# Layer A's inputs for quarters 2 to 4 from a transposed copy of x, normed in place on VectorE

## The chip, the cores and the metric

The kernel runs on one core of a Trainium2 chip. The metric is the device time of one execution in microseconds (us). An engine is named by what it is: TensorE (PE in the rows, PEld for its weight loads), VectorE (DVE), ScalarE (ACT), GpSimd (POOL) and SyncE (SP), whose queue issues all DMAs of this kernel.

## The reference

A trunk of two layers over 2048 tokens of width 1024, in f32. Layer A, which the change touches, begins with a norm over the features and a modulation, and everything after it reads that result with the features on the partitions:

```
def rms_norm(x, g):
    y = x * lax.rsqrt(jnp.mean(x * x, axis=-1, keepdims=True) + EPS)
    return y * g
def gmlp_layer(x, ...):
    h = rms_norm(x, norm_g) * (1 + scale) + shift
    u, v, z = jnp.split(h @ w_in, 3, axis=-1)
    ...
    return x + gate * (y @ w_out)
```

The shared K and V (h @ w_kv of layer A's output) and layer B (queries, attention over three dilations, w_out) follow.

## The kernel before

The tokens go in four quarters of 512, Q = 0 to 3, and each quarter runs through layer A, the K and V products (kv) and layer B's products (q, z) before the next. A product of 128x512 of output is summed in f32 precision out of three passes: operand and weight are split in a high and a low part (`split`, lines 272 and 273: ScalarE copies the high part, VectorE subtracts for the low one), and TensorE does high by high, high by low and low by high (`mm3`, line 301). One part of a quarter's work on the next quarter's input is recorded as a generator, a filler, whose steps are set between the matmuls at a rate (`tick`); each step's instructions then stand in their engines' queues at the place where it was taken, and a scheduler may still move them. Engines run their queues in order, and so does SP.

The inputs of layer A for quarters 1, 2 and 3 (the second to the fourth; named by Q in tiles such as h_a and pt_a) come from such fillers:

- `make_h(1, ...)` for quarter 2 and `make_h(0, ...)` for quarter 1 are both appended during Q = 0, the first beside the K and V products and the second from `ahead`, beside layer B's.
- `make_hA(nxt, 3, ...)` for quarter 3 is appended during Q = 2, beside layer B's products.

Each loads its four x tiles (128 tokens by 1024, 512 KB each) into one tile `xa` of a pool with one buffer, squares them on ScalarE in halves (`sqj`, line 897 or 1052), gets the reciprocal root on GpSimd (`rstd_of`, line 263), scales the x tiles by it on ScalarE (line 905), and then transposes them on TensorE, 32 transposes of 128x128 to a quarter (`pt_a`, line 915, or 861 in `norm_T`). VectorE applies the modulation as it copies the transposes from PSUM (line 917 or 870, 128x256 at a time), and the result h goes to DRAM (`hh`, `hd`). For quarters 1 and 3 it is also split: ScalarE copies the high part and GpSimd subtracts for the low one (lines 922 and 923, 872 and 876).

Four buffers of a pool `cb` with five, tag xin, hold the residual tiles xr of the quarter's own output while layer A's output product (pd_o, with weights w_o) fills them; their squares (xo, line 1358), the norm's reciprocal root r_b, the scaling on VectorE (line 1373) and the transposes `pt_b` (line 981) lead to hkh and hkl, the operands of kv. The residual goes to DRAM by `x1d`.

Of the kernel before, what the change touches and what calls it, by code (L numbers as in the profile page):

```python
# [34 lines left out]
@with_exitstack  # L35
def trunk(ctx, tc, out, x, c, a_ada_w, a_ada_b, a_norm_g, a_w_in, a_sgu_g, a_w_spatial,
          a_b_spatial, a_w_out, kv_ada_w, kv_ada_b, kv_norm_g, w_kv, k_norm_g, b_ada_w,
          b_ada_b, b_norm_g, b_w_in, b_q_norm_g, b_w_out, w_uz):
    nc = tc.nc
    x = x[0]  # L40
    out = out[0]
# [10 lines left out]
    bp = ctx.enter_context(tc.tile_pool(name="bp", bufs=2))  # L52
    sp = ctx.enter_context(tc.tile_pool(name="sp", bufs=4))
# [16 lines left out]
    hd = dp.tile([2, P, KT, 256], F32, name="hd")  # L70
    hh = dp.tile([2, P, KT, QT], F32, name="hh")
# [776 lines left out]
    def bigr(nm):  # L848
        return big.tile([P, KT, QT], F32R, tag="big", name=nm)

    def norm_T(xts, pr, outs, nm, ks=range(0, KT, 2), act=False):

        tok = slice(pr * 256, pr * 256 + 256)
        pts = {}
        for oi, (hh, hl, a, b) in enumerate(outs):
            for k2 in ks:
                if oi == 0:
                    pts[k2] = pst(f"pt_{nm}{k2}").rearrange("p (k t) -> p k t", k=2)
                    for kk in range(2):
                        for i in range(2):  # L860
                            last = nc.tensor.transpose(pts[k2][:, kk, i * P:(i + 1) * P],
                                                       xts[i][:, (k2 + kk) * P:(k2 + kk + 1) * P], ident)
                h = evt(f"h_{nm}{k2}_{oi}").rearrange("p (k t) -> p k t", k=2)
                for kk in range(2):
                    k = k2 + kk
                    if act or (oi == 1):
                        nc.scalar.activation(h[:, kk, :], pts[k2][:, kk, :], AF.Identity,
                                             scale=a[:, k:k + 1], bias=b[:, k:k + 1])
                    else:
                        nc.vector.tensor_scalar(h[:, kk, :], pts[k2][:, kk, :], a[:, k:k + 1],  # L870
                                                b[:, k:k + 1], ALU.mult, ALU.add)
                nc.scalar.activation(hh[:, k2:k2 + 2, tok], h, AF.Copy)
                if len(outs) == 1:
                    nc.sync.dma_start(hd[pr, :, k2:k2 + 2, :], h)
                e = nc.vector if oi == 0 and len(outs) > 1 else nc.gpsimd
                e.tensor_tensor(hl[:, k2:k2 + 2, tok], h,
                                hh[:, k2:k2 + 2, tok].bitcast(F32), ALU.subtract)
        return last

    def op_tile(nm, pool=big):  # L880
        t = pool.tile([P, 2, 4, QT], F32R, tag="big", name=f"op{nm}")
        return t[:, 0], t[:, 1]

    def make_h(half, aff, ops):

        Q = 1 + half
        xb = one.tile([P, TPQ, D], F32, tag="big", name=f"xa{Q}")
        xts = [xb[:, t, :] for t in range(TPQ)]
        for t in range(TPQ):
            nc.sync.dma_start(xts[t], x[(Q * TPQ + t) * P:(Q * TPQ + t + 1) * P, :])  # L890
        yield
        sq = sp.tile([P, 16], F32, tag="sqa", bufs=1, name=f"sqa{Q}")
        for t in range(TPQ):
            yield
            for h in range(2):
                j = evt(f"sqj{Q}{t}{h}")
                nc.scalar.activation(j, xts[t][:, h * 512:(h + 1) * 512], AF.Square,
                                     accum_out=sq[:, 4 * h + t:4 * h + t + 1])
        yield
        nc.gpsimd.tensor_tensor(sq[:, 8:12], sq[:, 0:4], sq[:, 4:8], ALU.add)  # L900
        r = rstd_of(sq[:, 8:12], TPQ, D, f"r_a{Q}")
        yield
        yield
        for t in range(TPQ):
            nc.scalar.activation(xts[t], xts[t], AF.Copy, scale=r[:, t:t + 1])
            yield
        for pr in range(2):
            tok = slice(pr * 256, pr * 256 + 256)
            for k2 in range(0, KT, 2):
                pt = pst(f"pt_a{Q}{pr}{k2}").rearrange("p (k t) -> p k t", k=2)  # L910
                h = evt(f"h_a{Q}{pr}{k2}").rearrange("p (k t) -> p k t", k=2)
                for kk in range(2):
                    k = k2 + kk
                    for i in range(2):
                        nc.tensor.transpose(pt[:, kk, i * P:(i + 1) * P],
                                            xts[2 * pr + i][:, k * P:(k + 1) * P], ident)
                    nc.vector.tensor_scalar(h[:, kk, :], pt[:, kk, :], aff[0][:, k:k + 1], aff[1][:, k:k + 1],
                                            ALU.mult, ALU.add)
                nc.sync.dma_start(hh[half, :, k2:k2 + 2, tok], h)
                if ops:  # L920
                    hi, lo = (o[:, k2 % 4:k2 % 4 + 2, tok] for o in ops[k2 // 4])
                    nc.scalar.activation(hi, h, AF.Copy)
                    nc.gpsimd.tensor_tensor(lo, h, hi.bitcast(F32), ALU.subtract)
                yield

    def sums_h(ops, n):

# [111 lines left out]
    def make_hA(res, Q, aff):  # L1039
        hA = (bigr(f"hAh{Q}"), bigr(f"hAl{Q}"))  # L1040
        res["hA"] = hA
        xb = one.tile([P, TPQ, D], F32, tag="big", name=f"xa{Q}")
        xts = [xb[:, t, :] for t in range(TPQ)]
        for t in range(TPQ):
            nc.sync.dma_start(xts[t], x[(Q * TPQ + t) * P:(Q * TPQ + t + 1) * P, :])
        yield
        sq = sp.tile([P, 16], F32, tag="sqa", bufs=1, name=f"sqa{Q}")
        for t in range(TPQ):
            yield
            for h in range(2):  # L1050
                j = evt(f"sqj{Q}{t}{h}")
                nc.scalar.activation(j, xts[t][:, h * 512:(h + 1) * 512], AF.Square,
                                     accum_out=sq[:, 4 * h + t:4 * h + t + 1])
        yield
        nc.gpsimd.tensor_tensor(sq[:, 8:12], sq[:, 0:4], sq[:, 4:8], ALU.add)
        r = rstd_of(sq[:, 8:12], TPQ, D, f"r_a{Q}")
        yield
        yield
        for t in range(TPQ):
            nc.scalar.activation(xts[t], xts[t], AF.Copy, scale=r[:, t:t + 1])  # L1060
            yield
        for pr in range(2):
            for k2 in range(0, KT, 2):
                norm_T(xts[2 * pr:2 * pr + 2], pr, [hA + aff], f"a{Q}_{pr}_", (k2,))
                yield

    def sums_A(Q, hA, m):

# [804 lines left out]
    outs = []  # L1873
# [187 lines left out]
    hA, m, sqv, ends = begin(affa)  # L2061
# [13 lines left out]
    for Q in range(NQ):  # L2075
# [40 lines left out]
        if Q == 2:  # L2116
            hA = nxt["hA"]
# [28 lines left out]
```

## Time and profile before

| what | us |
|---|---|
| runs of before: lowest, median, highest | 2903.33, 2909.21, 2909.3 |
| the profiled execution | 2910.12 |
| its span in the profile | 2908.3 |
| TensorE busy | 2851.9 (98%) |
| VectorE, ScalarE, GpSimd busy | 76%, 56%, 28% |

The span runs from the first to the last instruction in the profile of one execution, at a granted clock of 0.998. Busy time is the union of an engine's instructions. TensorE's idle time is thus only 56 us in all, spread over the span.

### The profile page before, as it was taken

How to read it: one execution, taken by the hardware profiler on the slowest of the kernel's cores; microseconds unless marked ns; L12 is line 12 of the kernel's file. 1: busy time of each engine (PE TensorE's matmuls, PEld its weight loads, DVE VectorE, ACT ScalarE, POOL GpSimd, SP SyncE). 2: the span in 40 equal slices, each digit the busy share in tenths (PEclk: the TensorE clock that was granted, in tenths of full speed). 3: DMA queues.
4: the chain of work that ended last, by engine and by line, in shares of the span. 5: the costliest groups of instructions: out<-in, count | busy, mean ns of one | idle time of the engine just before them, and what ended most of it. 6: DMA issues, size and time to landing. Idle time of an engine off the chain costs nothing.

```text
span 2908.3 us, 45236 instructions
## 1 busy us (share of the span) xinstructions
PE 2851.9 (98%) x14450; PEld 2386.6 (82%) x14450; DVE 2205.5 (76%) x4104; ACT 1639.2 (56%) x3335; POOL 819.7 (28%) x1085
## 2 busy tenths in 40 slices
PE   8999999999999999999999999999999999999999
PEld 5788888877888888878888788888888888888887
DVE  6887667786696789967777877789779676888782
ACT  4324345666556666545654557667666357776441
POOL 1067422330031025003315134115335121122312
PEclk9999999999999999999999999999999999999999
DMA  9899856887874555797888787955447867789653
GB/s 320 289 334 343 286 194 206 273 297 268 293 270 161 200 170 181 241 330 240 301 289 298 238 302 258 299 181 168 151 129 259 319 217 232 235 274 334 223 172 111
DMA packets 388209, 718.74 MB, mean 247 GB/s; under 512 B 42010, under 2 KB 121084, under 8 KB 387588
## 3 DMA queue, kind: packets, MB, share of 16 engines
q1 hardware_dynamic: 387972, 715.87, 73.1%
q8 instruction: 114, 1.87, 0.3%
q14 instruction: 123, 1.01, 0.1%
HBM read 541.52 MB, written 174.20 MB: 246 GB/s over the span
## 4 chain that ended last, share of the span: by engine, by line
PE 79%; DVE 6%; DMA 5%; ACT 4%; issue 4%; POOL 1%; SPq 0%; POOLq 0%; ACTq 0%; DVEq 0%
PE pd_kv L301 8%; PE po L1844 4%; PE pd_o L301 3%; PE pd_v L301 2%; PE pd_z L345 2%; PE pd_z L344 2%; PE pd_z L343 2%; PE pd_u L343 2%; PE pd_u L345 2%; PE pd_u L344 2%; PE pd_o3a L301 1%; PE pd_v3b L301 1%; DMA qt<-qd 1%; PE pf L2035 1%; PE pf L2037 1%
## 5 line engine op out<-in xcount | busy, mean ns | idle before, releaser
L301 PE MATMUL pd_kv<-w_kv,hkh 128*128 128x512 f32 x672 | 209.4, 392 | 2.2 <-DVE w_kv L273 2.1
L1844 PEld LDWEIGHTS po<-kv,pT 128*128 128x128 f32 x1200 | 148.8, 193 | 15.1 <-POOL pT L1819 4.4
L1844 PE MATMUL po<-kv,pT 128*128 128x128 f32 x1200 | 152.2, 277 | 6.3 <-ACT pT L1690 2.5
L301 PEld LDWEIGHTS pd_kv<-w_kv,hkh 128*128 128x128 f32 x672 | 125.0, 188 | 29.3 <-DVE w_kv L273 2.9
L301 PE MATMUL pd_kv<-w_kv,hkl 128*128 128x512 f32 x336 | 130.9, 390 | 0.0
L1607 POOL TENSOR_SCALAR s_q<-s_q 128x4 f32<-128x4 f32 x96 | 25.3, 264 | 350.5 <-DVE s_q L1606 276.3
L1784 ACT ACTIVATE pr<-pr,stat,rt 128x256 f32<-128x256 f32 (+1 forms) x192 | 104.2, 544 | 27.0 <-DVE stat L1778 18.9
L1463 POOL TENSOR_SCALAR vc<-vc,rvh 128x256 f32<-128x256 f32 x64 | 66.8, 1060 | 182.4 <-DMA vc<-vh 128.0
L272 ACT ACTIVATE w_q<-raw_q 128x512 fp32r<-128x512 f32 x144 | 88.2, 627 | 46.8 <-PE pd_kv L301 12.4
L273 DVE TENSOR_TENSOR w_q<-raw_q,w_q 128x512 fp32r<-128x512 f32 x144 | 96.2, 692 | 20.2 <-ACT w_q L272 19.3
L2035 PE MATMUL pf<-wo,yb 128*128 128x512 f32 x256 | 104.5, 408 | 0.2 <-ACT yb L1998 0.2
L343 PE MATMUL pd_u<-hAh,w_u 128*128 128x512 f32 x256 | 103.5, 404 | 0.0
L343 PE MATMUL pd_z<-hAh,w_z 128*128 128x512 f32 x256 | 102.8, 402 | 0.0
L2037 PE MATMUL pf<-wo,yb 128*128 128x512 f32 x256 | 100.6, 393 | 0.0
L345 PE MATMUL pd_z<-hAh,w_z 128*128 128x512 f32 x256 | 100.3, 392 | 0.0
L345 PE MATMUL pd_u<-hAh,w_u 128*128 128x512 f32 x256 | 100.2, 391 | 0.0
L2036 PE MATMUL pf<-wo,yb 128*128 128x512 f32 x256 | 100.0, 391 | 0.0
L344 PE MATMUL pd_u<-hAl,w_u 128*128 128x512 f32 x256 | 99.9, 390 | 0.0
L344 PE MATMUL pd_z<-hAl,w_z 128*128 128x512 f32 x256 | 99.9, 390 | 0.0
L1784 ACT ACTIVATE st_pr<-st_pr,stat,rt 128x256 f32<-128x256 f32 (+1 forms) x128 | 73.5, 576 | 31.7 <-DVE stat L1781 18.5
L1792 POOL TENSOR_TENSOR dg<-pr,ident 128x256 f32<-128x256 f32 x38 | 30.8, 812 | 201.1 <-ACT pr L1784 138.3
L1819 POOL TENSOR_TENSOR pT<-pT,dg 128x256 f32<-128x256 f32 x76 | 62.7, 829 | 79.1 <-DVE pT L1818 73.6
(1476 smaller groups left out, 8985.1 us busy)
## 6 DMA issues: line engine op xcount, KB each, us to landing
raw_q<-in_b_w_in_dram SPq DMA_DIRECT2D x144, 256.0 KB, 3.6
qt<-qd SPq DMA_DIRECT2D x96, 260.0 KB, 3.4
od<-ot SPq DMA_DIRECT2D x96, 256.0 KB, 3.1
w_o<-wtd SPq DMA_DIRECT2D x48, 512.0 KB, 5.7
raw_kv<-in_w_kv_dram SPq DMA_DIRECT2D x84, 256.0 KB, 3.5
kv<-kvd SPq DMA_DIRECT2D x75, 256.0 KB, 5.3
raw_u<-in_a_w_in_dram SPq DMA_DIRECT2D x64, 256.0 KB, 4.4
wt<-st_cw SPq DMA_DIRECT2D x64, 256.0 KB, 5.4
```

Source lines behind the costliest of these rows:

```text
L272: nc.scalar.activation(hi, src, AF.Copy)
L273: nc.vector.tensor_tensor(lo, src, hi.bitcast(F32), ALU.subtract)
L301: last_mm[0] = nc.tensor.matmul(pt, a, u[:, w, :], start=f, stop=e, skip_group_check=more)
L343: nc.tensor.matmul(pts[i], wh, hh[:, k, :], start=k == 0, stop=False)
L344: nc.tensor.matmul(pts[i], wh, hl[:, k, :], start=False, stop=False)
L345: nc.tensor.matmul(pts[i], wl, hh[:, k, :], start=False, stop=k == KT - 1)
L1463: nc.gpsimd.tensor_scalar(v[:, c, :], v[:, c, :], rvh[:, i:i + 1], None, ALU.mult)
L1784: nc.scalar.activation(pr[:, i, :], pr[:, i, :], AF.Exp, bias=mneg[:, i:i + 1], scale=u["rt"][:, h:h + 1], accum_out=lsum[:, i:i + 1])
L1844: nc.tensor.matmul(po[:, h * P:(h + 1) * P], u["pT"][h // hp][:, h % hp, j, :], u["kv"][:, j, kh, 1, :], start=j == 0, stop=j == nk - 1)
L2035: nc.tensor.matmul(pt, yb[:, 0, k, :], w_[:, 0, :], start=k == 0, stop=False)
L2036: nc.tensor.matmul(pt, yb[:, 0, k, :], w_[:, 1, :], start=False, stop=False)
L2037: nc.tensor.matmul(pt, yb[:, 1, k, :], w_[:, 0, :], start=False, stop=k == KT - 1)
```

## The change

A second copy of x, transposed on the host (features by tokens), is passed as `x_t`. One generator `normed_T` takes the place of the bodies of `make_h` and `make_hA`. It still loads the x tiles, now one at a time into five-buffer or two-buffer pools and only for their squares, which overwrite them. It loads the quarter of `x_t` into `xT` (512 features on 128 partitions by 8 by 512 tokens, in the one-buffer pool). GpSimd scales the identity by the reciprocal root of each x tile; TensorE multiplies ones by these diagonal tiles, which puts the 512 roots on every partition; ScalarE copies them to `rr`. VectorE multiplies each 128x512 slice of `xT` by `rr` in place and applies the modulation to it from SBUF. The stores and the split of the result stay, per feature block of 512 tokens instead of per pair of blocks and half of the tokens. `norm_T` goes, as do the transposes.

```
-    def norm_T(xts, pr, outs, nm, ks=range(0, KT, 2), act=False):
-        ...
     def make_h(half, aff, ops):
-        Q = 1 + half
-        xb = one.tile([P, TPQ, D], F32, tag="big", name=f"xa{Q}")
-        ...
-        for t in range(TPQ):
-            nc.scalar.activation(xts[t], xts[t], AF.Copy, scale=r[:, t:t + 1])
-            yield
-        for pr in range(2):
-            tok = slice(pr * 256, pr * 256 + 256)
-            for k2 in range(0, KT, 2):
-                pt = pst(f"pt_a{Q}{pr}{k2}").rearrange("p (k t) -> p k t", k=2)
-                h = evt(f"h_a{Q}{pr}{k2}").rearrange("p (k t) -> p k t", k=2)
-                for kk in range(2):
-                    k = k2 + kk
-                    for i in range(2):
-                        nc.tensor.transpose(pt[:, kk, i * P:(i + 1) * P],
-                                            xts[2 * pr + i][:, k * P:(k + 1) * P], ident)
-                    nc.vector.tensor_scalar(h[:, kk, :], pt[:, kk, :], aff[0][:, k:k + 1], aff[1][:, k:k + 1],
-                                            ALU.mult, ALU.add)
+    def normed_T(Q, aff, tile_of, put):
+        xT = one.tile([P, KT, QT], F32, tag="big", name=f"xT{Q}")
+        sq = sp.tile([P, 16], F32, tag="sqa", bufs=1, name=f"sqa{Q}")
+        xts = {}
+        def load(t):
+            xts[t] = tile_of(t)
+            nc.sync.dma_start(xts[t], x[(Q * TPQ + t) * P:(Q * TPQ + t + 1) * P, :])
+        load(0)
+        yield
+        for t in range(TPQ):
+            if t + 1 < TPQ:
+                load(t + 1)
+            yield
+            nc.scalar.activation(xts[t], xts[t], AF.Square, accum_out=sq[:, t:t + 1])
+        for k in range(0, KT, 2):
+            nc.sync.dma_start(xT[:, k:k + 2, :], x_t[k * P:(k + 2) * P, Q * QT:(Q + 1) * QT]
+                              .rearrange("(k p) t -> p k t", p=P))
+        yield
+        r = rstd_of(sq[:, 0:TPQ], TPQ, D, f"r_a{Q}")
+        yield
+        dg = evt(f"rd{Q}").rearrange("p (t c) -> p t c", t=TPQ)
+        for t in range(TPQ):
+            nc.gpsimd.tensor_scalar(dg[:, t, :], ident, r[:, t:t + 1], None, ALU.mult)
+        one_ = evt(f"on{Q}")[:, 0:P]
+        nc.gpsimd.memset(one_, 1.0)
+        yield
+        yield
+        pr = pst(f"pr_a{Q}")
+        for t in range(TPQ):
+            nc.tensor.matmul(pr[:, t * P:(t + 1) * P], one_, dg[:, t, :], start=True, stop=True)
+        rr = bp.tile([P, QT], F32, tag="bc", name=f"rr{Q}")
+        nc.scalar.activation(rr, pr, AF.Copy)
+        yield
+        for k in range(KT):
+            nc.vector.tensor_tensor(xT[:, k, :], xT[:, k, :], rr, ALU.mult)
+            h = evt(f"h_a{Q}{k}")
+            nc.vector.tensor_scalar(h, xT[:, k, :], aff[0][:, k:k + 1], aff[1][:, k:k + 1], ALU.mult, ALU.add)
+            put(k, h)
+            yield
+    def make_h(half, aff, ops):
+        def put(k, h):
+            nc.sync.dma_start(hh[half, :, k, :], h)
+            if ops:
+                hi_lo(*(o[:, k % 4, :] for o in ops[k // 4]), h)
+        return normed_T(1 + half, aff, lambda t: cb.tile([P, D], F32, tag="xin", name=f"xa{half}{t}"), put)
     def make_hA(res, Q, aff):
+        def put(k, h):
+            nc.sync.dma_start(hd[:, :, k, :].rearrange("c p t -> p c t"), h.rearrange("p (c t) -> p c t", c=2))
+            hi_lo(hA[0][:, k, :], hA[1][:, k, :], h)
+        return normed_T(Q, aff, lambda t: ap_.tile([P, D], F32, tag=("kT", "qT")[t % 2], bufs=1, name=f"xa{Q}{t}"), put)
```

The x tiles of `make_h` are named by half and tile: xa10 to xa13 belong to quarter 2, xa00 to xa03 to quarter 1.

Three pieces of the queues show what moves. On SP, near the end of layer A's output product of Q = 0 (o01, its second half of columns), the loads of the first weights of kv (raw_kv02) stood in a row before, with the stores of the first two residual tiles behind:

```order
L280 DMA raw_kv02_0_2_3682<-in_w_kv_dram 128x512
L280 DMA raw_kv02_0_3_3687<-in_w_kv_dram 128x512
L280 DMA raw_kv02_0_4_3692<-in_w_kv_dram 128x512
L280 DMA raw_kv02_0_5_3697<-in_w_kv_dram 128x512
L1363 DMA x1d_90<-xr0_0_2853 128x1024
L1363 DMA x1d_90<-xr0_1_2854 128x1024
L280 DMA raw_kv02_0_6_3702<-in_w_kv_dram 128x512
L280 DMA raw_kv02_0_7_3707<-in_w_kv_dram 128x512
```

At the same place of the changed kernel's SP queue:

```order
L280 DMA raw_kv02_0_2_3682<-in_w_kv_dram 128x512
L864 DMA xa11_4147<-in_x_dram 128x1024
L280 DMA raw_kv02_0_3_3687<-in_w_kv_dram 128x512
L280 DMA raw_kv02_0_4_3692<-in_w_kv_dram 128x512
L280 DMA raw_kv02_0_5_3697<-in_w_kv_dram 128x512
L864 DMA xa12_4156<-in_x_dram 128x1024
L864 DMA xa13_4195<-in_x_dram 128x1024
L864 DMA xa00_4782<-in_x_dram 128x1024
L1328 DMA x1d_90<-xr0_0_2853 128x1024
L1328 DMA x1d_90<-xr0_1_2854 128x1024
L280 DMA raw_kv02_0_6_3702<-in_w_kv_dram 128x512
```

Four loads of x tiles have come in, three of them in a row ahead of the stores and of the last two raw_kv02 loads. Of the pool's five buffers four hold xr0, so that these loads use the fifth, one after another: by the semaphores of the built program, xa12 waits for the square of xa11, xa13 for that of xa12, and xa00 for that of xa13.

On ScalarE, at the end of the same product's weight splits (w_o01), before:

```order
L272 ACTIVATE w_o01_1_6_3467<-raw_o01_1_6_3468 128x512
L272 ACTIVATE w_o01_1_7_3472<-raw_o01_1_7_3473 128x512
L272 ACTIVATE w_kv02_0_0_3671<-raw_kv02_0_0_3672 128x512
L1358 ACTIVATE xo0_1_0_3531,sq10_0_2861<-xr0_0_2853 128x512
L1358 ACTIVATE xo0_1_1_3541,sq10_1_2862<-xr0_1_2854 128x512
```

And in the changed kernel:

```order
L272 ACTIVATE w_o01_1_6_3467<-raw_o01_1_6_3468 128x512
L272 ACTIVATE w_o01_1_7_3472<-raw_o01_1_7_3473 128x512
L872 ACTIVATE xa11_4147,sqa2_4132<-xa11_4147 128x1024
L872 ACTIVATE xa12_4156,sqa2_4132<-xa12_4156 128x1024
L872 ACTIVATE xa13_4195,sqa2_4132<-xa13_4195 128x1024
L272 ACTIVATE w_kv02_0_0_3671<-raw_kv02_0_0_3672 128x512
L1323 ACTIVATE xo0_1_0_3531,sq10_0_2861<-xr0_0_2853 128x512
L1323 ACTIVATE xo0_1_1_3541,sq10_1_2862<-xr0_1_2854 128x512
```

Three whole squares now stand ahead of the first split of kv's weights and of the squares of the residual.

On TensorE, in the matmuls of o01 that end just before kv02, the first transposes of the residual tile xr0_0 stood here before:

```order
L301 MATMUL pd_o01_2_3369<-w_o01_1_4_3457,yh04_2475 128x512
L981 MATMUL pt_b0_1_0_3569<-ident_134,xr0_0_2853 128x128
L981 MATMUL pt_b0_1_2_3579<-ident_134,xr0_0_2853 128x128
L981 MATMUL pt_b0_1_4_3589<-ident_134,xr0_0_2853 128x128
L981 MATMUL pt_b0_1_6_3599<-ident_134,xr0_0_2853 128x128
L301 MATMUL pd_o01_2_3369<-w_o01_1_4_3457,yh04_2475 128x512
```

And in the changed kernel:

```order
L301 MATMUL pd_o01_2_3369<-w_o01_1_4_3457,yh04_2475 128x512 x2
L301 MATMUL pd_o01_2_3369<-w_o01_1_4_3457,yl04_2476 128x512
L301 MATMUL pd_o01_3_3370<-w_o01_1_4_3457,yh04_2475 128x512 x2
L301 MATMUL pd_o01_3_3370<-w_o01_1_4_3457,yl04_2476 128x512
L965 MATMUL pt_b0_1_0_3569<-ident_134,xr0_0_2853 128x128
L965 MATMUL pt_b0_1_2_3579<-ident_134,xr0_0_2853 128x128
L965 MATMUL pt_b0_1_4_3589<-ident_134,xr0_0_2853 128x128
L965 MATMUL pt_b0_1_6_3599<-ident_134,xr0_0_2853 128x128
```

They stand five matmuls later; the transposes of xr0_1 behind them stand six matmuls later, and the first matmul of kv02 follows the same matmuls as before.

## Rows read from the trace of the kernel before

**Rows 1.** The page's head: span; each engine's busy us, share, instructions.

```profile
span 2908.3 us, 45236 instructions
...
PE 2851.9 (98%) x14450; PEld 2386.6 (82%) x14450; DVE 2205.5 (76%) x4104; ACT 1639.2 (56%) x3335; POOL 819.7 (28%) x1085
```

**Rows 2.** Windows of 20 us: each engine's busy us (instructions), clock, DMA share, GB/s.

```profile
480.00:500.00 20.00, 20.00 (x98) 16.22 (x97) 19.39 (x35) 10.24 (x17) 9.94 (x21) 1.00 0.67 218
580.00:600.00 20.00, 18.87 (x89) 14.84 (x87) 19.86 (x32) 12.19 (x21) 13.62 (x22) 1.00 0.75 241
620.00:640.00 20.00, 18.72 (x87) 15.02 (x86) 18.57 (x29) 11.81 (x20) 3.27 (x2) 1.00 0.93 313
1640.00:1660.00 20.00, 20.00 (x90) 16.57 (x89) 19.47 (x34) 16.38 (x32) 0.00 (x0) 1.00 0.48 138
```

**Rows 3.** Timeline of TensorE in 1789 to 1813: start, us, line, operation.

```profile
1795.13 5.60 PE L301 MATMUL pd_q20a<-w_q20t,hob 128*128 128x512 f32 x24
1800.57 1.52 PE L301 MATMUL pd_q20b<-w_q20t,hob 128*128 128x512 f32 x6
...
1806.50 1.53 PE L301 MATMUL pd_q20a<-w_q,hob 128*128 128x512 f32 x6
```

**Rows 4.** The tile pt_a: ns min/median/max, first and last; TensorE's wait.

```profile
L915 PE MATMUL pt_a<-ident,xa x64: 270/272/330, 485.7 to 630.1; 128*128 128x128 f32 x64
...
L861 PE MATMUL pt_a<-ident,xa x32: 270/272/273, 1801.9 to 1842.4; 128*128 128x128 f32 x32
...
  PE pt_a L915: 2.4, 3
```

**Rows 5.** Timeline of TensorE in 1606 to 1612.

```profile
1607.34 3.68 PE L1844 MATMUL po<-kv,pT 128*128 128x128 f32 x16 [2.04 <-POOL pT L1819]
```

**Rows 6.** The page's costliest groups, GpSimd: busy us, mean ns, idle before.

```profile
L1463 POOL TENSOR_SCALAR vc<-vc,rvh 128x256 f32<-128x256 f32 x64 | 66.8, 1060 | 182.4 <-DMA vc<-vh 128.0
```

**Rows 7.** Groups of VectorE by form in 480 to 640: busy us, mean ns.

```profile
L917 DVE TENSOR_SCALAR h_a<-pt_a,affa,affa 128x256 f32<-128x256 f32 x32 | 17.0, 540 | 4.9 <-PE pt_a L915 4.8
...
L273 DVE TENSOR_TENSOR w_z0bt<-raw_z0bt,w_z0bt 128x512 fp32r<-128x512 f32 x16 | 12.4, 799 | 3.1 <-ACT w_z0bt L272 3.1
...
L273 DVE TENSOR_TENSOR w_z0b<-raw_z0b,w_z0b 128x512 fp32r<-128x512 f32 x12 | 9.7, 834 | 0.8 <-ACT w_z0b L272 0.8
...
L273 DVE TENSOR_TENSOR ops<-fh,ops 128x512 fp32r<-128x512 f32 x2 | 2.5, 1238 | 0.0
L942 DVE TENSOR_TENSOR fh<-fh 128x512 f32<-128x512 f32 x3 | 2.1, 687 | 1.0 <-DMA fh<-hh 0.9
```

**Rows 8.** The line L1373 by itself: ns min/median/max.

```profile
L1373 DVE TENSOR_SCALAR xr<-xr,r_b x4: 746/746/753, 401.1 to 419.8; 128x1024 f32<-128x1024 f32 x4
```

**Rows 9.** Groups of ScalarE by form in 440 to 580: busy us, mean ns.

```profile
L897 ACT ACTIVATE sqj<-xa 128x512 f32<-128x512 f32 x16 | 9.9, 622 | 0.0
...
L905 ACT ACTIVATE xa<-xa,r_a 128x1024 f32<-128x1024 f32 x8 | 9.2, 1145 | 3.5 <-POOL r_a L267 3.4
...
L626 ACT ACTIVATE st_q01u<-pd_q01b 128x512 f32<-128x512 f32 x2 | 1.2, 600 | 0.2
```

**Rows 10.** Timeline of ScalarE in 385 to 408; in brackets the idle before.

```profile
398.10 0.63 ACT L272 ACTIVATE w_kv<-raw_kv 128x512 fp32r<-128x512 f32 x1 [11.11 <-PE pd_o L301]
```

**Rows 11.** Timeline of SP's queue in 378 to 414.

```profile
382.46 5.62 SPq L280 DMA_DIRECT2D raw_kv<-in_w_kv_dram  x6
```

**Rows 12.** DMA issues, whole trace: count, KB each, median us to landing.

```profile
xr<-in_x_dram SPq DMA_DIRECT2D x16, 512.0 KB, 4.1
...
xa<-in_x_dram SPq DMA_DIRECT2D x12, 512.0 KB, 6.6
```

**Rows 13.** Timeline of VectorE in 399 to 410.

```profile
401.12 0.75 DVE L1373 TENSOR_SCALAR xr<-xr,r_b 128x1024 f32<-128x1024 f32 x1
```

**Rows 14.** Timeline of TensorE in 400 to 420.

```profile
402.21 0.60 PE L981 MATMUL pt_b<-ident,xr 128*128 128x128 f32 x4
...
409.33 0.62 PE L301 MATMUL pd_kv<-w_kv,hkh 128*128 128x512 f32 x2
```

More of the change, by code (lines that the diff above doesn't have):

```diff
@@ L37, in trunk @@
           a_b_spatial, a_w_out, kv_ada_w, kv_ada_b, kv_norm_g, w_kv, k_norm_g, b_ada_w,
-          b_ada_b, b_norm_g, b_w_in, b_q_norm_g, b_w_out, w_uz):
+          b_ada_b, b_norm_g, b_w_in, b_q_norm_g, b_w_out, w_uz, x_t):
     nc = tc.nc
@@ L849, in bigr @@
         return big.tile([P, KT, QT], F32R, tag="big", name=nm)
-    def norm_T(xts, pr, outs, nm, ks=range(0, KT, 2), act=False):
-        tok = slice(pr * 256, pr * 256 + 256)
[L854 to L858, printed above, removed]
-                    for kk in range(2):
-                        for i in range(2):
[L861 to L864, printed above, removed]
-                    k = k2 + kk
[L866 to L878, printed above, removed]
     def op_tile(nm, pool=big):
@@ L882, in op_tile @@
         return t[:, 0], t[:, 1]
-    def make_h(half, aff, ops):
-        Q = 1 + half
-        xb = one.tile([P, TPQ, D], F32, tag="big", name=f"xa{Q}")
-        xts = [xb[:, t, :] for t in range(TPQ)]
-        for t in range(TPQ):
-            nc.sync.dma_start(xts[t], x[(Q * TPQ + t) * P:(Q * TPQ + t + 1) * P, :])
+    def normed_T(Q, aff, tile_of, put):
[7 more added lines that the diff above has]
+        yield
+        for t in range(TPQ):
+            if t + 1 < TPQ:
[5 more added lines that the diff above has]
+                              .rearrange("(k p) t -> p k t", p=P))
@@ L891, in make_h @@
         yield
-        sq = sp.tile([P, 16], F32, tag="sqa", bufs=1, name=f"sqa{Q}")
+        r = rstd_of(sq[:, 0:TPQ], TPQ, D, f"r_a{Q}")
+        yield
+        dg = evt(f"rd{Q}").rearrange("p (t c) -> p t c", t=TPQ)
         for t in range(TPQ):
-            yield
[L895 to L898, printed above, removed]
@@ L899, in make_h @@
-        yield
-        nc.gpsimd.tensor_tensor(sq[:, 8:12], sq[:, 0:4], sq[:, 4:8], ALU.add)
-        r = rstd_of(sq[:, 8:12], TPQ, D, f"r_a{Q}")
+            nc.gpsimd.tensor_scalar(dg[:, t, :], ident, r[:, t:t + 1], None, ALU.mult)
+        one_ = evt(f"on{Q}")[:, 0:P]
+        nc.gpsimd.memset(one_, 1.0)
         yield
         yield
+        pr = pst(f"pr_a{Q}")
         for t in range(TPQ):
-            nc.scalar.activation(xts[t], xts[t], AF.Copy, scale=r[:, t:t + 1])
-            yield
-        for pr in range(2):
-            tok = slice(pr * 256, pr * 256 + 256)
-            for k2 in range(0, KT, 2):
-                pt = pst(f"pt_a{Q}{pr}{k2}").rearrange("p (k t) -> p k t", k=2)
-                h = evt(f"h_a{Q}{pr}{k2}").rearrange("p (k t) -> p k t", k=2)
-                for kk in range(2):
-                    k = k2 + kk
-                    for i in range(2):
-                        nc.tensor.transpose(pt[:, kk, i * P:(i + 1) * P],
-                                            xts[2 * pr + i][:, k * P:(k + 1) * P], ident)
-                    nc.vector.tensor_scalar(h[:, kk, :], pt[:, kk, :], aff[0][:, k:k + 1], aff[1][:, k:k + 1],
-                                            ALU.mult, ALU.add)
[L919 to L924, printed above, removed]
@@ L926, in sums_h, with hi_lo @@
+    def hi_lo(hi, lo, h):
+        nc.scalar.activation(hi, h, AF.Copy)
+        nc.gpsimd.tensor_tensor(lo, h, hi.bitcast(F32), ALU.subtract)
+    def make_h(half, aff, ops):
[4 more added lines that the diff above has]
+        return normed_T(1 + half, aff, lambda t: cb.tile([P, D], F32, tag="xin", name=f"xa{half}{t}"), put)
     def sums_h(ops, n):
@@ L1041, in make_hA @@
         res["hA"] = hA
-        xb = one.tile([P, TPQ, D], F32, tag="big", name=f"xa{Q}")
-        xts = [xb[:, t, :] for t in range(TPQ)]
-        for t in range(TPQ):
[L1045 to L1065, printed above, removed]
+        def put(k, h):
+            nc.sync.dma_start(hd[:, :, k, :].rearrange("c p t -> p c t"), h.rearrange("p (c t) -> p c t", c=2))
+            hi_lo(hA[0][:, k, :], hA[1][:, k, :], h)
+        return normed_T(Q, aff, lambda t: ap_.tile([P, D], F32, tag=("kT", "qT")[t % 2], bufs=1, name=f"xa{Q}{t}"), put)
     def sums_A(Q, hA, m):
@@ L2137 @@
                           kind="ExternalInput").ap() for n in _INS]
+    x_t = np.ascontiguousarray(np.asarray(inputs["x"])[0].T)
+    arrays["in_x_t_dram"] = x_t
     ins.append(nc.dram_tensor("in_w_uz_dram", w_uz.shape, mybir.dt.from_np(w_uz.dtype),
                               kind="ExternalInput").ap())
+    ins.append(nc.dram_tensor("in_x_t_dram", x_t.shape, mybir.dt.from_np(x_t.dtype), kind="ExternalInput").ap())
     outs = [nc.dram_tensor(f"out_{i}_dram", shape, mybir.dt.from_np(np.dtype(dt)),
```

## The prediction

> **What bounds the kernel now.** I read the page first: TensorE is busy for 2851.9 of the 2908.3 us, VectorE for 76% [rows 1]. Only TensorE's own work, or a wait that it newly gets, can move the time; what another engine saves counts only where TensorE stood waiting for it. Then I took the windows of the places that the change touches [rows 2]: where the fourth quarter's inputs begin (1640 to 1660) TensorE is busy for the whole 20 us and in 480 to 500 too, but in 580 to 600 it loses 1.1 us and in 620 to 640 1.3 us, with VectorE busy for 19.86 and 18.57. So two kinds of place exist: full TensorE, where work taken from it comes back one for one, and full VectorE, where its own pace decides.
>
> **Removed from TensorE.** The reader is to see what a transpose costs in a stream of matmuls, which is not its own duration. A product of 24 matmuls starts at 1795.13 and the next at 1800.57: 5.44 us, 227 ns a matmul. The one from 1800.57 has four transposes between its sixth and seventh matmul, and the next starts at 1806.50: 5.93 us [rows 3]. Four transposes cost 0.49 us, 0.12 each, though each lasts 272 ns by itself [rows 4]. There are 64 for the second and third quarters and 32 more for the fourth, so 96 x 0.12 to 0.13: **-12.0 us**. With them goes the wait for VectorE to free their PSUM tile, 2.4 us in three places [rows 4]: **-2.4 us**.
>
> **Added to TensorE.** Three groups of four f32 128x128 matmuls, ones by the diagonal tile. The nearest row is 16 matmuls of that shape in 3.68 us [rows 5], 0.23 each: 12 x 0.23, **+2.7 us**. By a transpose's price it would be 1.5. Net on TensorE: -11.7 us.
>
> Each group waits for GpSimd, which makes four scaled identities of 128x128 and a tile of ones. A GpSimd multiply of 128x256 takes 1.06 us [rows 6], so half that, 0.53, is an estimate for one and 2.1 us for four. For the third quarter the group stands in a product that begins shortly before 480, right after GpSimd's work on r_a2 and a q norm; the cost lies between 0 and 2.1. For the other two the group comes several us after the sums, so nothing. I take **+0.5**, nearer nothing, since the scaling and squares that leave ScalarE let its part of the chain come earlier.
>
> **VectorE.** Per quarter 16 multiply-adds from PSUM go, at 0.54 us; 8 products of two SBUF tiles of 128x512 come, 0.69 us each by the row of that shape, and 8 multiply-adds from SBUF [rows 7]. The last have no row of their shape; one of 128x1024 from SBUF takes 0.746 [rows 8], so half of it, 0.37, is the lower bound, and 0.54, the PSUM form of half the size, the upper. The sum is 8.5 to 9.8 against 8.6: nothing to +1.2 of busy time, before overlap. But both new kinds read SBUF beside GpSimd, which makes the low halves at the same places. Rows show what this does: w_z0b takes 834 and w_z0bt 799 ns where the undisturbed product takes 687, and one pair took 1238 [rows 7]. For the quarter whose stretch is 580 to 640, 8 x (0.82 - 0.69) is **+1.0** where VectorE is full; elsewhere TensorE was full with VectorE at most 97% busy, and I take nothing.
>
> **ScalarE** loses work: 8 half squares at 0.62 and 4 scalings at 1.15, 9.6 us a quarter, for 4 whole squares (1.2) and one copy of 0.6, 5.4 us [rows 9]. It does not bound TensorE in these places, so the sum has nothing for it. The 2 MB more per quarter are hidden too: 6 MB in all, they are read where the queues are partly idle, the chain below apart.
>
> **A new wait, in the first quarter.** The order lists show the loads xa11, xa12, xa13 and xa00 in one slot of five (the residual tiles hold the other four): each waits for the square of the one before, and on ScalarE the three squares stand ahead of the first w_kv02 split and of the squares of xo0_1. Before, ScalarE had idled 11.1 us until 398.10 there [rows 10]; the question is whether three loads and squares fit. Six raw_kv loads were issued from 382.46 in 5.62 us, 0.94 apart [rows 11]; xa11 goes out behind the third, 385.3. A 512 KB load takes 4.1 us for a tile from x by itself and 6.6 where four were issued in a row [rows 12]. For xa11, beside raw_kv, I take 5.5, then a square of 1.3 (2 x 0.62, and its sum read): 392.1. The other two run alone, 4.1 + 1.3 each: 402.9. So ScalarE resumes 4.8 us late.
>
> Behind it wait the squares, their sums, GpSimd's r_b, VectorE's scaling of xr (from 401.12, done at 401.87 [rows 13]), the transposes pt_b on TensorE, hkh and hkl, and the first kv02 matmul at 409.33 [rows 14]. pt_b started at 402.21 and now stands five matmuls later, 1.13 us: 403.34. Slack 403.34 - 401.87 = 1.5 us, so TensorE stalls for 4.8 - 1.5: **+3.3 us**. The lower bound is 0, if each load takes 3.5 us or less; the upper, with 6.6 for each load, is a resumption at 409.0, a delay of 10.9 and a stall of 9.4. I take the middle value since nothing else uses the queues then. On the SP queue two stores of x1d and raw_kv02_0_6 and 7 stand behind xa00; TensorE needs those weights 36 matmuls, 8.2 us, after kv02 begins, so they cost nothing. If ScalarE's stall grew past that, these would be late next.
>
> For the fourth quarter the chain has two slots, and its last two squares come on ScalarE behind two weight splits of kv21; TensorE is full in 1640 to 1660 [rows 2]. I take nothing, at most 1 us.
>
> **Sum.** 2910.12 (the profiled run; its span of 2908.3 and 1.8 around it) - 11.7 + 0.5 + 1.0 + 3.3 = 2903.2. The profiled run lies 0.9 above the median of 2909.21, so **2902 us**, 0.25% faster. Some 0.2%, 5.8 us, is what a measurement of this kernel can tell from no change.
>
> **Rivals.** *The load chain costs more.* Each of the three loads takes 6.6 us, stall 9.4 and not 3.3: 2909.3, less 0.9, 2908.4. For it: the median of xa's loads; against it: those were issued four in a row.
>
> *The load chain is hidden* and nothing new waits: the full 11.7, 2897.5. For it: 11 us of idle ScalarE; against it: one slot.
>
> *VectorE becomes the bound: slower.* If GpSimd holds back each new operation as it held that pair, a product costs 1.24 and a multiply-add its 0.37 plus the same 0.55, 0.92: 17.3 us a quarter in place of 8.6, +8.7. In 580 to 640 VectorE has at most 1.4 idle us in 20 and in 480 to 500 0.6 [rows 2], so in three quarters up to 26 us less some 6 of idle time: +20, of which 1.0 is in the sum already: 2921. It decides against the change from about 13 us of uncovered VectorE work, 0.27 us for each of the 48 new operations. Against it: the means of that stretch, 0.80 and 0.83, are far below 1.24. The Trainium skill, SBUF — State Buffer, section Who interferes with whom, says that a VectorE instruction with two SBUF inputs contends with a GpSimd instruction that reads SBUF, and that tensor_scalar in a two-port mode contends too, while an instruction with at most one SBUF input outside those modes does not; whoever comes second is blocked for the whole instruction. By that rule both new kinds can be held, and the removed ones could not; rows 7 agree that products are held now and then, and no run here yet shows the multiply-adds.
>
> *Transposes were covered by other work* and removing them gives nothing; -2.4, +2.7, +0.5, +1.0 and +3.3 stay: 2915.2, less 0.9, 2914.3. Against it: the 5.93 beside 5.44.
>
> **Chances.** Forecast 0.45 (its own range 2899 to 2906); hidden chain 0.20; costlier chain 0.20; VectorE 0.12; covered 0.03. The range reaches from the hidden chain, with 1.5 less for the ones matmuls, to the costlier chain with 1 to 2 more: 2896 to 2911. Faster than 2903.4 is the hidden chain and most of the forecast's case: 0.53; within 0.2% the rest of it and the costlier chain: 0.34; slower mostly VectorE's: 0.13.
>
> **What would show it.** Products in the three stretches at 5.44 us with no transposes, and no wait for h_a: the first term. ScalarE idle at about 387 to 403 waiting for xa11 to xa13 and TensorE idle by some 3 us at pt_b: the fourth. VectorE's new rows at 0.69 and 0.37 to 0.54: if their means are above 0.9 and TensorE waits for splits by VectorE, the third rival. What would make it wrong is another order of waits that I don't see in the lists: a TensorE wait above 2 us anywhere other than at pt_b.

## The result and the profile after

The changed kernel is **slower**, by 0.3%: 2914.99 us median of 22 runs beside 2906.53 for the kernel before, a ratio of 1.0028 with a 95% interval of 1.0018 to 1.0038. That is +8 us where -7 was forecast, outside the forecast range.

The profiled execution of the changed kernel happened to be the shortest of its 22 (2904.79 us, span 2902.7), shorter than the profiled one of before [rows 1]. One profile against one profile would have said "faster". So the same kernel was profiled once more (run e1 below), with a span of 2913.7 us that is near its median; its rows are read here unless another run is named. The head of its page:

```profile
span 2913.7 us, 45106 instructions
...
PE 2849.1 (98%) x14378; PEld 2384.9 (82%) x14378; DVE 2204.8 (76%) x4104; ACT 1630.5 (56%) x3302; POOL 840.5 (29%) x1097
```

TensorE is busy for 2.8 us less than in [rows 1] and the span is 5.4 us longer. Its idle time thus grew from 56.4 to 64.6 us, by 8.2. The removed transposes less the new matmuls are 9.3 us of busy time by the prediction's terms; that only 2.8 are missing leaves an estimate of some 6.5 us that its work lost by running at the lower clock in some stretches. So the loss is about as much clock as waits. Where TensorE stood waiting, in the list of its waits (us in total, times, longest):

```profile
PE pt_b L965 <- DVE xr L1338: 5.9, 1, 5.9
PE pd_vh4a L301 <- ACT pd_vh4a L1373: 4.4, 3, 3.1
...
PE pd_v3a L301 <- ACT w_v L272: 2.1, 1, 2.1
```

The first and the third are new. The second is not the wait of before at 698 us, of 2.1 and 0.7: its 3.1 us stand at an earlier product, where TensorE had not waited, and only 0.6 and 0.7 are left at the old place. The product before, and in e1:

```profile
662.93 5.60 PE L301 MATMUL pd_vh4a<-w_vh4t,ops 128*128 128x512 f32 x24
```

```profile
666.28 7.35 PE L301 MATMUL pd_vh4a<-w_vh4t,ops 128*128 128x512 f32 x24 [3.07 <-ACT pd_vh4a L1373]
```

ScalarE begins the copies that free its PSUM tile at 664.54, before at 660.15. The product also takes 1.75 us longer, at a granted clock of 0.78 and 0.88 in two windows of 5 us from 665.

**The first place, pt_b.** ScalarE, from 386 us (idle before each in brackets):

```profile
392.08 1.06 ACT L872 ACTIVATE xa<-xa 128x1024 f32<-128x1024 f32 x1 [4.36 <-DMA xa<-in_x_dram]
...
396.87 1.06 ACT L872 ACTIVATE xa<-xa 128x1024 f32<-128x1024 f32 x1 [3.63 <-DMA xa<-in_x_dram]
...
401.68 1.06 ACT L872 ACTIVATE xa<-xa 128x1024 f32<-128x1024 f32 x1 [3.66 <-DMA xa<-in_x_dram]
...
403.26 0.61 ACT L1323 ACTIVATE xo<-xr 128x512 f32<-128x512 f32 x1
```

Three loads, each behind the square of the one before, as the order lists said. SP's queue at the same time, then GpSimd's last step of r_b for the first tile, then VectorE's first scaling of xr:

```profile
386.44 0.46 SPq L864 DMA_DIRECT2D xa<-in_x_dram  x1
...
393.26 9.92 SPq L864 DMA_DIRECT2D xa<-in_x_dram  x3
403.28 0.86 SPq L1328 DMA_DIRECT2D x1d<-xr  x2
```

```profile
404.52 0.55 POOL L267 TENSOR_TENSOR r_b<-r_b,mhalf 128x1 f32<-128x1 f32 x1
```

```profile
408.92 0.75 DVE L1338 TENSOR_SCALAR xr<-xr,r_b 128x1024 f32<-128x1024 f32 x1 [2.50 <-DMA x1d<-xr]
```

The root for the first tile is ready at 405.07 (404.52 + 0.55), but the scaling starts at 408.92. It writes xr in place, so it waits until the store x1d has read xr, and that store was issued at 403.28, behind xa00 on SP. VectorE idles 2.50 us for it. Before, it was issued at 398.06, and the scaling started at 401.12 [rows 13]:

```profile
398.06 0.93 SPq L1363 DMA_DIRECT2D x1d<-xr  x2
```

TensorE in e1 at this place, and its windows of 5 us (busy us of PE, PEld, DVE, ACT, POOL, then the granted clock, DMA share, GB/s):

```profile
409.82 1.09 PE L965 MATMUL pt_b<-ident,xr 128*128 128x128 f32 x4 [5.93 <-DVE xr L1338]
...
411.56 0.63 PE L301 MATMUL pd_o<-w_o,yl 128*128 128x512 f32 x1
411.99 1.05 PE L301 MATMUL pd_o<-w_o,yh 128*128 128x512 f32 x2
412.84 0.63 PE L301 MATMUL pd_o<-w_o,yl 128*128 128x512 f32 x1
```

```profile
400.00:405.00 5.00, 3.89 (x18) 2.88 (x16) 0.93 (x3) 3.32 (x8) 0.67 (x2) 1.00 0.41 95
405.00:410.00 5.00, 0.18 (x1) 0.21 (x2) 2.38 (x4) 1.66 (x4) 1.67 (x3) 0.84 1.00 376
410.00:415.00 5.00, 5.00 (x17) 4.13 (x17) 2.23 (x4) 0.63 (x1) 0.00 (x0) 0.50 0.52 179
415.00:420.00 5.00, 5.00 (x27) 4.28 (x26) 4.90 (x10) 3.97 (x9) 0.00 (x0) 0.98 0.71 226
```

The reader is to see the second cost of a wait. In 410 to 415 TensorE is busy for all 5 us, but at a granted clock of 0.50: 1.2 in place of 2.4 GHz. Three matmuls from 411.56 to 412.84 take 1.28 us, 427 ns each, where 227 is the pace [rows 3]. The clock fell inside the wait (0.84 in 405 to 410) and was back at 0.98 by 415 to 420. From the first pt_b to the first kv02 matmul TensorE takes 8.48 us; before it took 7.12, and five matmuls of that, 1.13 us, now stand ahead. So the lower clock costs another 2.5 us. The first kv02 matmul starts at 418.30, before at 409.33 [rows 14]: 9.0 us later. (In the shorter first profile this place cost 5.1 us of wait and a start at 416.04.) The Trainium skill, TensorE: Matmul & The Clock Gate, Part 1: The HAM clock gate, says that the throttled state is the default and that activity releases it; these rows agree as to the direction.

**The second place, pd_v3a.** Where the fourth quarter's first layer A product begins, TensorE waits again, and the clock falls again (0.72 and 0.59 in two windows of 5 us from 1850):

```profile
1844.65 5.60 PE L301 MATMUL pd_z2bb<-w_z2b,hob 128*128 128x512 f32 x24
1852.32 0.80 PE L301 MATMUL pd_v3a<-w_v,hAh 128*128 128x512 f32 x1 [2.07 <-ACT w_v L272]
1853.74 0.80 PE L301 MATMUL pd_v3a<-w_v,hAh 128*128 128x512 f32 x1 [0.62 <-DVE w_v L273]
```

Before, it did not wait there, and the sums of m came after the first splits of w_v:

```profile
1853.42 0.62 PE L301 MATMUL pd_v3a<-w_v,hAh 128*128 128x512 f32 x2
```

```profile
1854.95 1.22 DVE L1086 TENSOR_TENSOR m<-m 128x1024 f32<-128x1024 f32 x1
```

VectorE and ScalarE ahead of that split in e1:

```profile
1845.88 1.22 DVE L1051 TENSOR_TENSOR m<-m 128x1024 f32<-128x1024 f32 x1 [4.62 <-DMA m<-hd]
```

```profile
1848.39 1.06 ACT L272 ACTIVATE sA<-m 128x1024 fp32r<-128x1024 f32 x1 [7.01 <-DVE m L1052]
...
1851.66 2.17 ACT L272 ACTIVATE w_v<-raw_v 128x512 fp32r<-128x512 f32 x4
```

The sums m of h's blocks, read back from hd, and their splits sA stood behind the first w_v splits before; they stand ahead of them now, and wait for a DMA. The change stores h per feature block of 512 tokens, so all of hd is complete only at the end, and the four loads of m go out together.

**What the prediction expected and the trace has.** In the fourth quarter's products with no transposes each product of 24 takes 5.44 us (1795.69 to 1801.13 to 1806.57), where it took 5.93 with four of them [rows 3]:

```profile
1795.69 5.60 PE L301 MATMUL pd_q20a<-w_q20t,hob 128*128 128x512 f32 x24
1801.13 5.60 PE L301 MATMUL pd_q20b<-w_q20t,hob 128*128 128x512 f32 x24
1806.57 5.60 PE L301 MATMUL pd_q20a<-w_q,hob 128*128 128x512 f32 x24
```

From the first kv02 matmul (9.0 us late) to the first of vh4a, 641.17 before and 641.30 now, TensorE wins 8.8 us back, for two quarters.

### The profile page after: what moved, and what is told of

The parts are those of the page before. It is cut to its first block, busy times and chain, and to the rows that moved or that the text cites. A ratio compares the mean times of both kernels' runs of the same rounds, so it can differ in the third digit from the quotient of the medians.

```text
span 2902.7 us, 45106 instructions
## 1 busy us (share of the span) xinstructions
PE 2845.0 (98%) x14378; PEld 2381.9 (82%) x14378; DVE 2199.5 (76%) x4104; ACT 1629.5 (56%) x3302; POOL 838.8 (29%) x1097
## 4 chain that ended last, share of the span: by engine, by line
PE 78%; DMA 8%; DVE 6%; issue 3%; ACT 3%; POOL 2%; SPq 0%; POOLq 0%; DVEq 0%; ACTq 0%
PE pd_kv L301 7%; PE po L1809 4%; PE pd_o L301 2%; PE pd_u L343 2%; PE pd_u L345 2%; PE pd_u L344 2%; PE pd_z L345 2%; PE pd_z L344 2%; PE pd_z L343 2%; PE pd_v L301 2%; PE pd_v3a L301 1%; PE pd_v3b L301 1%; PE pd_o3a L301 1%; PE pf L2002 1%; PE pf L2000 1%
## 5 line engine op out<-in xcount | busy, mean ns | idle before, releaser
L272 ACT ACTIVATE w_z<-raw_z 128x512 fp32r<-128x512 f32 x64 | 39.8, 628 | 81.8 <-PE pd_z L345 37.2
```

Source lines behind the costliest of these rows:

```text
L272: nc.scalar.activation(hi, src, AF.Copy)
```

## The experiments

The table counts quarters as the recorded expectations do, from the first to the fourth. All times are medians in us; the ratio is to the kernel before, run in the same group, with a 95% interval. Each carries some 3 us of uncertainty, so places are compared in the traces and totals by the ratios.

| run | what | ratio (interval) |
|---|---|---|
| e1 | the change again | 1.0028 (1.0017 to 1.0039) |
| e2 | second and third quarters alone | 1.0026 (1.0016 to 1.0037) |
| e3 | fourth quarter alone | 1.0015 (1.0006 to 1.0024) |
| e4 | x tiles in xT's buffer, squares hoisted | 1.0125 (1.0110 to 1.0140) |
| e5 | the same, half squares late | 1.0041 (1.0029 to 1.0053) |
| e6 | e5, sums of m later | 1.0028 (1.0018 to 1.0037) |
| e7 | the change, sums of m later | 1.0031 (1.0019 to 1.0043) |
| e8 | the change, xa00 later | 1.0057 (1.0043 to 1.0070) |
| e9 | squares in ScalarE's gap | 0.9990 (0.9981 to 0.9999) |
| e10 | e9, sums of m later | 0.9985 (0.9976 to 0.9995) |
| e11 | before again, one profile | 2910.94 us |
| e12 | before, 48 transposes left out | 0.9981 (0.9969 to 0.9993) |

**e1, the change again.** No edit.

> The changed kernel as it is, for a second profile beside the kernels of this group. The theory: in the first quarter three loads and squares in one buffer slot hold ScalarE, and the fourth load holds the SP queue and with it the stores of x1d, which the in-place scaling of xr waits for; TensorE then stalls at pt_b for 5 us or more and runs at the lower clock for some us after; a second stall of 3 us with a drop of the clock stands at pd_v3a, 1845 us, where four loads of m and VectorE's sums of it now stand ahead of the weight splits. Both must be seen again, and the ratio must be near 1.003. The rival (VectorE held back by GpSimd at the new instructions) expects the loss spread over 480 to 640 and 1780 to 1830, with TensorE waiting for VectorE there.

Both waits were there, as shown above, and VectorE's stretch in 580 to 640 held TensorE up nowhere: it was busy for 20.00 us in each window of 20, where it had lost 1.1 and 1.3 [rows 2]. The rival falls as the cause.

**e2 and e3, one part each.** In e2 `make_hA` is that of before, in e3 `make_h` is.

> Quarters 2 and 3 as in the change, quarter 4 (make_hA) as before. The theory: the stall at pt_b stays and the one at pd_v3a goes; 64 transposes and the 2.4 us of waits less the ones matmuls give back 8, the stall at pt_b with its clock takes 8 to 15: 0 to 7 us slower than before. The rival, by its two quarters of three: 5 us slower, spread over the new instructions.

> Quarter 4 as in the change, quarters 2 and 3 as before. The theory: no stall at pt_b beyond the 0.5 us of before, the one at pd_v3a stays; 32 transposes less four ones matmuls give 3.1, that stall with its clock takes 5: 2 us slower than before. The rival: a third of the loss, 3 us slower, and no wait of TensorE at pd_v3a for splits behind m.

Each has its own wait and not the other's: in e2 TensorE waits 8.6 us at pt_b and not at pd_v3a, in e3 1.5 and 0.9 at pd_v3a and nothing new at pt_b. So each part is slower than before by itself. e2 loses 7.6 us by its ratio, all that the whole change does, and e3 4.4; both are above what the first theory allowed from one profile (0 to 7, and 2). The profiled execution of e3 was the shortest of its 12 and shows the two waits without a fall of the clock, so it does not show where the total's 4.4 us lie.

**e4, no slot chain.**

```
+        xts = [xT[:, 2 * t:2 * t + 2, :].rearrange("p k t -> p (k t)") for t in range(TPQ)]
-            xts[t] = tile_of(t)
```

> All three quarters as in the change, but the x tiles are loaded into the buffer of xT, squared there, and x_t is loaded over them, so that no x tile waits for a slot among the residual tiles and no load stands on SP ahead of x1d. The theory: no stall at pt_b, the one at pd_v3a stays; 11.7 less 5, so 5 to 8 us faster than before and 13 to 16 faster than the changed kernel. The rival: VectorE has the same instructions, so the loss of the changed kernel stays, 8 us slower than before.

The forecast missed by 40 us, by an accident of the edit: with nothing to hold them, the squares of the third quarter's tiles were set at the head of ScalarE's queue, ahead of the first modulations, and waited for their load there:

```profile
47.53 1.06 ACT L866 ACTIVATE xT<-xT 128x1024 f32<-128x1024 f32 x1 [27.69 <-DMA xT<-in_x_dram]
```

TensorE waited 26.2 us for it. From there to kv02 nothing more was lost (26.1 us late at the first matmul of o and at the first of kv02): without the chain pt_b waits 0.5 us as before. The total says nothing on the theory.

**e5 and e6, the squares in halves again.** As e4, but squared into evacuation tiles as before; e6 also queues the sums of m behind the first v3 splits:

```
+            for h in range(2):
+                j = evt(f"sqj{Q}{t}{h}")
+                nc.scalar.activation(j, xts[t][:, h * 512:(h + 1) * 512], AF.Square,
+                                     accum_out=sq[:, 4 * h + t:4 * h + t + 1])
...
+        with tc.issue_after(hold[0].ins), tc.issue_after(hold[1].ins):
             late[0]()
```

> As the fourth run, x tiles in the buffer of xT, but squared in halves into the evacuation tiles as the kernel before did, so that the squares keep their place on ScalarE (in the fourth run they stood at the head of its queue, ahead of the first modulation, and TensorE lost 26 us at the start). The theory: no stall at pt_b, offset 0 at the first kv matmul; the stall at pd_v3a of 2 to 3 us with its clock stays: 11.7 less some 5.5, so 4 to 7 us faster than before. The rival (VectorE and GpSimd contend at the new instructions): as slow as the changed kernel.

> The run before this one, and VectorE's sums of m and the split sA behind it queued behind the last weight split of the first v3 product on VectorE and ScalarE. The theory: neither stall, 9 to 12 us faster than before. If the second stall was only a shift of a wait that comes later anyway, it is as fast as the run before this one.

pt_b waited 0.5 us as before, kv02 came 0.2 and 0.7 us earlier, and still both were slower than before. The wait had moved to the ones matmuls of the third quarter, whose diagonal tiles came late from GpSimd. It was not for want of the roots: r_a2 was there at 468.47, and the first tile starts at 478.95, behind a q norm that had itself waited for VectorE:

```profile
477.25 0.19 POOL L1570 TENSOR_SCALAR s_q<-s_q 128x4 f32<-128x4 f32 x1 [8.77 <-DVE s_q L1569]
```

Those sums follow work of ScalarE that had waited 2.86 us for a weight load (raw_q02t), and on SP such loads stand behind the last load of x_t, which went out at 466.39, after the last square. That this is how the late squares came to cost the wait is argued from these rows; no run tests it. The wait and the windows of e5:

```profile
PE pr_a L886 <- POOL on L881: 4.7, 1, 4.7
```

```profile
480.00:485.00 5.00, 1.43 (x6) 1.44 (x7) 2.98 (x5) 1.14 (x2) 4.75 (x10) 0.60 0.84 265
485.00:490.00 5.00, 5.00 (x20) 4.10 (x19) 3.41 (x6) 1.72 (x3) 0.38 (x2) 0.72 0.27 101
```

Again the clock falls with the wait, to 0.60 and 0.72 in these windows.

**e7, only the sums of m later.**

> The changed kernel with only the sums of m queued later. The theory: the stall at pd_v3a of 2 to 3 us and its clock go, 5 us less than the changed kernel, so 2 to 4 us slower than before; the stall at pt_b stays.

The wait at the start of pd_v3a went down to 0.3 us (one of 1.2 stands later, behind m), and the total did not follow: 1.0031 beside 1.0028. In the profiled execution the loads at pt_b were slower (7.9 us of wait, 2.0 more than in e1); whether that hides the gain in the median is not shown.

**e8, x1d ahead of xa00.**

```
+            with tc.issue_after(last_ld[0].ins) if Q == 1 else nullcontext():
                 nc.sync.dma_start(xts[t], x[(Q * TPQ + t) * P:(Q * TPQ + t + 1) * P, :])
```

> The changed kernel with the first load of quarter 2's x tiles (xa00) queued behind the last weight load traced before it, so that it no longer stands on SP ahead of the stores of x1d; the three squares on ScalarE stay where they are. If the store of x1d, which must have read xr before VectorE scales it in place, is what ends last, that scaling starts by 2 us earlier (404.5 to 405) and TensorE reaches kv02 some 3 us earlier than in the changed kernel; if ScalarE's delay alone counts, it starts at 407 as before this edit. In both cases a stall stays, since ScalarE is still 3 us late.

ScalarE resumed later here than in e1, since xa11 and xa13 took longer, so absolute times don't compare; the step does. The stores went out at 400.26, and VectorE's scaling no longer waits for them: the root is ready at 407.67 and the scaling starts at 408.34, 0.67 us after, where it was 3.85 us in e1 (405.07 to 408.92).

```profile
407.12 0.55 POOL L267 TENSOR_TENSOR r_b<-r_b,mhalf 128x1 f32<-128x1 f32 x1
```

```profile
408.34 0.75 DVE L1339 TENSOR_SCALAR xr<-xr,r_b 128x1024 f32<-128x1024 f32 x1
```

So the store on SP costs 2.5 us of the wait (VectorE's idle time for it in e1) to 3.2 us (3.85 less 0.67; in e1 one more weight split stands ahead of the scaling). This run was slower than e1 all the same, with 6.7 us of wait at pt_b and 3.1 and 0.9 at pd_v3a. In 500 to 645 TensorE also waits 2.3 us where it did not wait in e1, 1.6 of them for VectorE. Why its total is that much worse stays open.

**e9 and e10, squares where ScalarE idled.** The x tiles of the third quarter go into xT's buffer at the start and are squared whole behind the last w_o01 split; x_t is loaded over them later. e10 also has the sums of m later.

```
+        early = Q == 2
+                behind.enter_context(tc.issue_after(marks["o01_1_7"][1].ins))
+                for t in range(TPQ):
+                    load(t)
+                    nc.scalar.activation(xts[t], xts[t], AF.Square, accum_out=sq[:, t:t + 1])
...
+                behind.enter_context(tc.issue_after(marks["kv02_0_7"][0].ins))
```

> The changed kernel, but quarter 3's x tiles are loaded into xT's buffer at the start of the program and squared whole in the 11 us that ScalarE idles after the last split of w_o01, and the four pieces of x_t are loaded over them behind raw_kv02_0_7. Neither the load chain at pt_b nor late squares at pr_a are left; the stall at pd_v3a stays. The theory (each newly placed wait costs TensorE its length and a stretch at the lower clock behind it, and nothing else is lost): offset about 0 at the first kv matmul, -9 at vh4a, and 2 to 6 us faster than before at the end. The rival (VectorE's new instructions cost the time wherever they stand): 5 us or more slower.

> The run before this one with the sums of m queued behind the first v3 splits. The theory: neither stall; 6 to 11 us faster than before and 14 to 18 faster than the changed kernel. The rival: no faster than before.

Both are faster than before; e10 by 0.15%, at 2901.43 us beside 2907.06, and so the lowest ratio of the kernels here that compute the reference, 0.43% below the changed kernel (0.9985 / 1.0028). The squares fit in the gap: the first starts in e9 at 386.74, right behind the last w_o split, and TensorE waits 0.3 us at pt_b. With the same new VectorE instructions as in the changed kernel, the loss is gone (the intervals of e9 and of the change do not meet), which settles the rival. In e10 TensorE's waits at pd_v3a are 0.7 and 0.5 us in place of 3.6 and 0.7 in e9:

```profile
PE pd_vh4a L304 <- ACT pd_vh4a L1389: 4.6, 3, 2.7
...
PE pd_v3a L304 <- ACT w_v L272: 0.7, 1, 0.7
PE pd_v3a L304 <- DVE w_v L273: 0.5, 2, 0.3
```

The two intervals overlap, so the second place's price in the total is not resolved by this pair, only its price in the trace.

**e11 and e12, the kernel before.**

> The kernel before again, for a second profile: three to five stretches of 3.4 us at the lower clock, as in the first, if the profile shown is a usual one; fewer would put it at some 2903 us. No wait above 1 us at pt_b or pd_v3a under either theory.

> The kernel before with 48 of the 96 transposes left out (of each pair of feature blocks only the first is transposed, and VectorE modulates it twice, so h holds wrong values for every second block); every other instruction is there. It asks whether TensorE's work comes back one for one. If it does: 48 x 0.12, 6 us less, some of the 2.4 us of waits too, so 6 to 8 us faster than before. If what is won is given back at later waits that end when they did before (the first of them vh4a at 698 us): 2 to 4 us faster.

The second profile of before has a span of 2909.1 us: the first was a usual one, if on the long side. e12 won 0.19%, 5.5 us where TensorE's work alone gives 6, with an interval of 2 to 9. So removed work does come back in the total too, not only in the trace; the interval does not tell one for one (6 to 8) from partly given back (2 to 4).

## Why the prediction was wrong

The sign that it named itself came twice: a TensorE wait above 2 us elsewhere than at pt_b, 3.1 at vh4a and 2.1 at pd_v3a. Its rival of covered transposes gave 2914.3, close to the measured 2914.99, but by luck: the products at 5.44 us refute its mechanism. Its base, the median of three runs, lay 2.7 us above the 2906.53 of 22, which moves the forecast by as much and leaves its direction.

Its terms, by its own steps:

- **Removed transposes and h_a waits (-14.4), added matmuls (+2.7): right.** 8.8 us over two quarters against 8.6 (64 x 0.125, and 2.4, less 1.8), and 5.44 in place of 5.93 for each product. A group of ones matmuls costs 0.81 us (from 575.11 to the next at 575.92) where 0.91 was taken.
- **GpSimd ahead of the ones matmuls (+0.5): about right**, 0.21 us in e1, though a scaled identity took 0.81 us (mean of the eight in 480 to 660) where 0.53 was taken. e5 shows that the term had a cliff: the q norm ahead of the tiles began 5.4 us before TensorE came to the group in e1 and 1.6 before in e5, and there it was 4.7 and a fall of the clock.
- **VectorE (+1.0): too much.** TensorE waited for none of it. The products had a median of 0.684 us over all 24 and a mean of 0.779 in 480 to 660; the multiply-adds took 0.536 (median of 24), the upper of the two bounds. Both kinds took longer now and then (longest 1.78 and 0.89 us), and GpSimd paid more: its subtractions for the low half rose from a median of 1.34 to 1.74 us, the longest 4.03. The rule of the Trainium skill, SBUF — State Buffer, section Who interferes with whom, agrees with this so far; it just wasn't on TensorE's path in e1.
- **The load chain (+3.3): the mechanism right, the size far too small (8.6 measured).** The delay of ScalarE was forecast well, partly by luck: it reached the split just before the xo squares at 402.74, and the forecast had 402.9, but xa11 went out 1.1 us later (386.44, not 385.3) and each further load and square took 4.8 us, not 5.4. The step that failed is "they cost nothing", of the stores of x1d behind xa00: the prediction looked for who needs what SP held and named the weights, but not that the scaling in place must wait for the store. VectorE's 2.5 us of idle time for that store are in the wait of 5.9; the other 3.4 are what the chain alone was forecast to cost. And the prediction had no term for the clock: 2.5 us more.
- **The fourth quarter (+0, "at most 1"): the step that failed is that it looked at the start of that quarter's inputs only.** Where they end, the order of m and w_v had turned round. The wait of 2.7 us and the clock moved TensorE from 3.3 us ahead of the kernel before (1844.65 against 1847.98 for the last z product) to 2.7 behind at pd_v3b (1861.59 against 1858.87). Why the total of e7, where this wait is short, did not gain stays open.
- **Given back: the prediction had no term for it.** By vh4a TensorE has won back 8.8 us since kv02, and then it waits 3.1 us at a product that had not waited. The old wait at 698 shrinks from 2.8 to 1.3 us and its stretch at the lower clock goes; from 641 to the product at 711.41 (713.42 in e1) the changed kernel falls back by 1.9 us. e12, which only leaves transposes out, waits 1.4 us at the same product, so a part of this wait comes with TensorE's earlier arrival alone.

The sum by the first profile of before: -11.8 on TensorE (8.8 and 3.0 more in the fourth quarter), +8.6 at pt_b (9.0 less 0.4 that was late before it), +6.0 at pd_v3a, +1.9 at vh4a: +4.7, and the spans differ by 5.4. What stays open: by its ratio e10 wins 4 us and not the 11 of TensorE's terms. Its trace waits longer than that of before at vh4a, uh6y and po (4.6 for 2.8, 3.6 for 2.5 and 7.8 for 6.2 us in all), with stretches at the lower clock behind some of them, and such waits differ from one execution to the next (2902.7 and 2913.7 us for the two profiles of the changed kernel); which of them the earlier arrival causes was not separated. The larger total of e8 and the small effect of e7 may be of that kind; no run shows it.

## What to carry to other kernels

Where one engine is busy for 98% of the time, a new wait on it can cost more than work removed from it brings: its own length, and often half of a stretch for which the clock then stays down. Ahead of such a change, list every instruction that a moved load or square now stands in front of, on each queue, and ask of each store behind it who overwrites what it reads. Look at the end of the moved work as at its start, since a result that comes out in another order turns later queues round.

## What the runs showed of the hardware

- TensorE's granted clock fell in waits of 5.9 (e1), 4.7 (e5) and 2.1 us followed by 0.6 (e1, at pd_v3a), and stood at 0.50 in a full window of busy work behind the first. In e3 waits of 1.5 and 0.9 us at pd_v3a, and in e9 one of 2.4 at vh4a, left it at 1.00 in all windows of 5 us around. A wait's price is thus not fixed by its length.
- A multiply-add with two scalars of 128x512 from SBUF took 0.536 us (median of 24), where a multiply by one scalar of 128x1024 takes 0.746 [rows 8]: half the size, in another form, is 0.72 of the time, not half.
- Loads of 512 KB in the chain came to the next square's start in 4.8 us each (392.08, 396.87, 401.68), but the first, beside weight loads, took 5.6 us from issue to use in e1 and 8.2 in e2 (385.97 to 394.15).
